# Moving the low parts of u and the block sums of u from GpSimd to VectorE, and the last token tile's transposes by twelve matmuls, in a two-layer diffusion backbone on one core

## Chip, core, metric

One core of a Trainium2 chip runs the whole program as one launch. The metric is the device time of that launch in microseconds. TensorE is PE in the profile (its weight loads are PEld), VectorE is DVE, ScalarE is ACT, GpSimd is POOL, and SP is the queue that issues most DMAs.

## What is computed

One inference step of two layers for 128 context tokens and 512 latent tokens, 640 tokens of width 1024 that share the weights. Cut to what matters here:

```
for l in range(2):
    x = LN(a*x + 0.5*g1 * SwiGLU_1(x*(1+s1) + b1))      # d_ff 2816
    x = LN(a*x + g2 * W_out[RG-LRU | GQA | MLA](x*(1+s2) + b2))
    x = LN(a*x + 0.5*g3 * SwiGLU_2(x*(1+s3) + b3))

SwiGLU(u) = (silu(u @ w_gate) * (u @ w_up)) @ w_down
```

Everything is float32. The shifts, scales and gates come from a modulation product of the condition vector. The outputs are the tokens of both groups and the context tensors of each layer.

## The kernel before, in words

**Products.** A float32 product is made of three passes: each operand is split into a high part (rounded to the type that TensorE multiplies) and a low part (the operand less its high part), and `mm3` adds hi·hi, hi·lo and lo·hi in PSUM. Weights come by SP DMAs of 512 KB into `raw` (seven buffers); ScalarE casts the high part (L195, L1063) and VectorE subtracts to get the low part (L200, L1067).

**The stage input u.** u = x*(1+s)+b is held transposed as `uh` and `ul`, each two tiles of 128 x 4 x 640 (features by tokens). `ln_b(t)` makes token tile t of it: eight transposes on TensorE (L516) into a PSUM tile of tag `p2`; eight evacuations with scale and shift into `uf`, shared between VectorE (L521) and ScalarE (L523); then for each half of the features a cast to `uh` (ScalarE, L527) and `ul = uf - uh` (L529, GpSimd). `uf` has one buffer, so tile t+1 cannot be evacuated before the low parts of tile t are done. `p2` has three slots of two banks, shared with the accumulators of gate and up.

**Order of the stages.** f00 (first FFN of layer 0, `ffn_steps`), m0 (mixer), f01, f10, m1, f11; f01, f10 and f11 are the three that `ffn_fast` writes and that the diff reaches with all its parts. They start at 884, 1340 and 2128 us. At the end of a stage, the last part runs token tile by token tile: the products of tile t, VectorE's multiply and add (L1211, L1212) and statistics (L478), `ln_a(t)` (aggregate L485, L487; a power on GpSimd, L488; the factors, L502; the normalisation on ScalarE, L506, and VectorE, L508), then `modulate(t-1)`, that is `ln_b` of the tile before. So tile 4, the last, is left over: `end_tile` puts its `modulate` into `after_q`, and the next stage's first step calls it by `after_a()`.

**Start of a fast FFN.** `first()` in `ffn_fast` runs gate columns 0 to 383 (24 matmuls, token tiles 0 to 2), then `after_a()` (tile 4's transposes and the rest of `ln_b`), up columns 0 to 383 (24 matmuls), gate columns 384 to 639 (tiles 3 and 4), up columns 384 to 639. `mtile` yields after every 12 matmuls. The mixer's `first()` has the same form and its `after_a()` is not in the diff.

**Sums and the change to seven products.** From the fourth block of d_ff on, a fast FFN computes gate and up by seven half-size products on sums of the four blocks of u (two feature halves by two token halves). `sums()` runs behind the first three blocks as a background generator: `whole` adds `uh + ul` of a block (L990, eight per FFN on GpSimd, 128x640 each), VectorE adds and subtracts these (L997, L1002, L1003, L1009), ScalarE and VectorE split them again (L985, L986). `third()` then closes the `p2` pool, opens single-bank `pb` tiles and starts the products (L1091). The multiply of gate and up (L941) of the third block must be done before the pool can be swapped. `residual` (L2351, L2352) is more VectorE background work of this stretch.

**What sets the order on an engine.** When the program is built, a scheduler orders each engine's instructions: among those whose inputs it plans to be ready, the one that stands first in the program goes first, and `high_priority(offset=n)` counts an instruction as n places earlier (`SUMS` = 200 for the sums). On the chip each engine keeps that order, whatever comes late.

**Weights of the projections.** `run` executes a list of `Step`s. Before a step's body it finishes the step's own splits (high and low parts of its weights); while the body yields, it makes splits of the nearest following steps that have any: `near` holds the first `look` of them, and `cap` is how many splits may be made ahead in this step:

```
near = [todo[k] for k in range(i + 1, min(len(steps), i + 40)) if steps[k].splits][: s.look]
cap = s.cap
for more in s.body():
    cap += more or 0
    nxt = next((q for q in near if q), None)
    if nxt and cap and self.ahead and nxt[0].ready():
        nxt.popleft()()
        cap -= 1
```

The mixer's token-major projections (`tokens`) are steps of four splits each with cap 2; the last of them adds 2 by `yield 2`. They come in the order 1024, 1280, (1504, a `proj` of two splits), 512, 768, then the MLA weights (two splits), sixteen loads of modulation weights, and the output projection.

Of the kernel before, what the change touches and what calls it, by code (L numbers as in the profile page):

```python
# [18 lines left out]
P = 128  # L19
# [5 lines left out]
CUT = 384  # L25
# [44 lines left out]
LN_LAG = 1, 1  # L70
WOUT = (0,), (1,), (2, 3)
WCAP = 1
LOV = ()
FA = 1
FIN = ()
QP = 1
# [12 lines left out]
def f(ap):  # L89
    return ap.bitcast(F32)  # L90
# [20 lines left out]
class Kern:  # L111
# [398 lines left out]
    def ln_b(self, x, t, sp, bp, uh, ul):  # L510

        nc = self.nc
        g = 1 if t == 0 else 0
        pt = self.p2().rearrange("p a (b c) -> p (a b) c", c=P)
        for k in range(KT):
            nc.tensor.transpose(pt[:, k, :], x[:, k * P : (k + 1) * P], self.ident)  # L516
        uf = self.pp.tile([P, KT, P], F32, tag="uf", bufs=1, name=self.nm("uf"))
        for k in range(KT):
            s1, s2 = sp[:, g, k : k + 1], bp[:, g, k : k + 1]
            if k % 4 < EVAC[self.ln_idx[1] != 1]:  # L520
                nc.vector.tensor_scalar(uf[:, k, :], pt[:, k, :], s1, s2, op0=ALU.mult, op1=ALU.add)  # L521
            else:
                nc.scalar.activation(uf[:, k, :], pt[:, k, :], AF.Identity, bias=s2, scale=s1)  # L523
        for h in range(2):
            d = uh[h][:, :, t * P : (t + 1) * P]
            v = uf[:, 4 * h : 4 * h + 4, :]
            nc.scalar.copy(d, v)  # L527
            e = nc.vector if (t, h) in LOV else nc.gpsimd
            e.tensor_sub(ul[h][:, :, t * P : (t + 1) * P], v, f(d))  # L529

    def u_alloc(self):
        return [self.U([P, 4, TOK]) for _ in range(2)], [self.U([P, 4, TOK]) for _ in range(2)]
# [350 lines left out]
    def ffn_fast(self, l, j, mods):  # L883
# [8 lines left out]
        nc, I = self.nc, self.I  # L892
# [5 lines left out]
        def B(dt=F32):  # L898
            return env["pool"].tile([P, TOK], dt, tag="B", bufs=10, name=self.nm("b"))
# [7 lines left out]
        def SB(shape):  # L907
            return env["pool"].tile(shape, F32R, tag="S", bufs=6, name=self.nm("s"))
# [4 lines left out]
        def view(w, m):  # L913
            return w[l, j][:, fs(m)].rearrange("(k p) f -> p k f", p=P)
# [8 lines left out]
        def split_h(m, s):  # L923
            hh, hl = B(F32R), B(F32R)
            nc.scalar.copy(hh, s)
            nc.vector.tensor_sub(hl, s, f(hh))
            hs[m] = (hh, hl)


        def plain(m):  # L930
            g, u = {}, {}
            gl, gsp = self.weight(view(I["ffn_w_gate"], m), [P, KT, P], g, self.W)
            ul, usp = self.weight(view(I["ffn_w_up"], m), [P, KT, P], u, self.W)

            def silu(cut):
                for a, b in self.chunks(g["s"], g["ps"], cut):
                    nc.scalar.activation(a, b, AF.Silu)

            def hout(cut):
                for a, b in self.chunks(g["s"], u["ps"], cut):  # L940
                    nc.vector.tensor_mul(a, a, b)  # L941
                split_h(m, g["s"])

            def first():
                env["cm"] = self.tc.tile_pool(name=f"ffn{l}{j}", bufs=1, reuse_waits="tile")
                env["pool"] = env["cm"].__enter__()
                g["ps"], u["ps"] = self.p2(), self.p2()
                g["s"] = B()
                yield from self.mtile(g["ps"], g, 0, CUT)
                self.hold = True  # L950
                self.after_a()
                yield from self.mtile(u["ps"], u, 0, CUT)
                yield from self.mtile(g["ps"], g, 1, CUT)
                silu(CUT)
                env["sums"] = sums()
                self.bg.append(env["sums"])
                yield from self.mtile(u["ps"], u, 1, CUT)
                hout(CUT)

            def gate():  # L960
                g["ps"] = self.p2()
                g["s"] = B()
                for c in range(2):
                    yield from self.mtile(g["ps"], g, c)
                silu(HALF)

            def up():
                u["ps"] = self.p2()
                for c in range(2):
                    yield from self.mtile(u["ps"], u, c)  # L970
                hout(HALF)

            if m == 0:
                return [Step([gl, ul], gsp + usp, first)]
            return [Step([gl], gsp, gate), Step([ul], usp, up)]


        def sums():
            uh, ul = self.uh, self.ul
            env["S"] = {i: (SB([P, 4, HALF]), SB([P, 4, HALF])) for i in (1, 2, 4)}  # L980
            env["s3"] = []

            def put(i, t, ks):
                hi, lo = env["S"][i]
                nc.scalar.copy(hi[:, ks], t)  # L985
                nc.vector.tensor_sub(lo[:, ks], t, f(hi[:, ks]))  # L986

            def whole(h, ts, ks):
                t = B().rearrange("p (k n) -> p k n", k=2)
                nc.gpsimd.tensor_add(t, f(uh[h][:, ks, ts]), f(ul[h][:, ks, ts]))  # L990
                return t

            for r in range(2):
                ks = slice(2 * r, 2 * r + 2)
                with self.tc.high_priority(offset=SUMS):
                    t21, t22 = whole(0, H1, ks), whole(1, H1, ks)
                    nc.vector.tensor_add(t22, t21, t22)  # L997
                yield
                with self.tc.high_priority(offset=SUMS):
                    t11 = whole(0, H0, ks)  # L1000
                    put(1, t22, ks)
                    nc.vector.tensor_sub(t21, t11, t21)  # L1002
                    nc.vector.tensor_sub(t11, t22, t11)  # L1003
                yield
                env["s3"].append((t21, ks))
                with self.tc.high_priority(offset=SUMS):
                    t12 = whole(1, H0, ks)
                    put(2, t11, ks)
                    nc.vector.tensor_sub(t12, t12, t11)  # L1009
                    put(4, t12, ks)  # L1010
                yield
# [285 lines left out]
    def mixer_steps(self, l, mods):  # L1297
        nc, I, O = self.nc, self.I, self.O
# [741 lines left out]
        def proj(c0, post, first=None):  # L2040
            h = {}
            ld, sp = self.weight(I["w_in"][l][:, c0 : c0 + P].rearrange("(k p) f -> p k f", p=P), [P, KT, P], h, self.W)
            n = len(S)

            def body():
                h["ps"] = self.p2("pg" if n % 2 == 0 else "pu")
                for c in range(2):
                    yield from self.mtile(h["ps"], h, c)
                post(h["ps"])
                yield  # L2050

            return h, ld, sp, body
# [43 lines left out]
        def tokens(c0, evac, post, pre=lambda: None, pairs=0):  # L2096

            hd = [{}, {}]
            lds, sps = [], []
            for i in range(2):  # L2100
                ld, sp = self.weight(
                    I["w_in"][l][i * 512 : (i + 1) * 512, c0 : c0 + 256].rearrange("(k p) n -> p k n", p=P),
                    [P, 4, 256],
                    hd[i],
                    self.W,
                )
                lds.append(ld)
                sps += sp

            def part(pt, t, half):  # L2110
                ts = slice(t * P, (t + 1) * P)
                for k in range(4 * half, 4 * half + 4):
                    wh, wl = hd[half]["hi"][:, k % 4, :], hd[half]["lo"][:, k % 4, :]
                    xh, xl = self.uh[half][:, k % 4, ts], self.ul[half][:, k % 4, ts]
                    self.mm3(pt, xh, xl, wh, wl, k == 0, k == KT - 1)

            def body():
                pre()
                for t in range(NT - 2 * pairs):
                    pt = self.p1()[:, 0:256]  # L2120
                    part(pt, t, 0)
                    yield
                    part(pt, t, 1)
                    evac(t, pt)
                    yield
                if pairs:
                    pts = [self.p1()[:, 0:256] for _ in range(2)]
                    part(pts[0], NT - 2, 0)
                    yield
                    part(pts[1], NT - 1, 0)  # L2130
                    yield 2
                    for i in range(2):
                        part(pts[i], NT - 2 + i, 1)
                        evac(NT - 2 + i, pts[i])
                        yield
                post()
                yield

            return Step(lds, sps, body, 2)

        def kv_evac(t, pt):
            if t == 0:
# [31 lines left out]
        for c0, post in ((128, xa1), (384, ga1)):  # L2174
            h, ld, sp, body = proj(c0, post)
# [3 lines left out]
        h, ld, sp, body = proj(1504, bgpost(c_post))  # L2179
# [407 lines left out]
```

## Time and profile before

| | us |
|---|---|
| median of 3 runs | 2592.18 |
| lowest, highest | 2592.03, 2599.52 |
| profiled execution, its own time | 2593.82 |
| its span, first to last instruction | 2592.0 |
| PE busy | 2470.4 (95%) |
| DVE busy | 1887.8 (73%) |
| ACT busy | 1067.8 (41%) |
| POOL busy | 534.6 (21%) |

In the profile a row of the timeline gives start, duration, engine, line, operation, output and inputs by name, and in brackets how long the engine was idle before it and what ended that. The windows view gives for a stretch the busy time of each engine and the mean granted TensorE clock, 1.00 for 2.4 GHz throughout and 0.50 for 1.2 GHz. The waits view sums, over the span, the time that an engine stood idle before a line, by what ended the wait, with the count and the longest. Matmuls overlap in the pipeline, so the distance between starts, not the duration, is what one costs.

### The profile page before, as it was taken

To read this page: it belongs to the slowest core of one execution; us is meant where nothing else is said; L and a number is where in the kernel's file an instruction comes from. 1 tells how busy PE (TensorE), PEld (TensorE's weight loads), DVE (VectorE), ACT (ScalarE), POOL (GpSimd) and SP (SyncE) were. 2 spreads that over 40 slices of the span, in tenths; PEclk is the share of its full clock that TensorE was granted. 3 is DMA by queue.
4 is the path that set the end of the run, shared out by engine and by line. 5 is a ranking of instruction groups with operands and counts; after the bars stand their busy time and mean duration, and the time that the engine had idled before them with its cause. 6 is when DMAs were issued, how large, how long until landed. Compare 5 with 4: busy or idle time off the path is not lost. (4 is left out here: it accounts for less than half of the span.)

```text
span 2592.0 us, 40008 instructions
## 1 busy us (share of the span) xinstructions
PE 2470.4 (95%) x15804; PEld 2220.3 (86%) x15804; DVE 1887.8 (73%) x3087; ACT 1067.8 (41%) x1882; POOL 534.6 (21%) x463
## 2 busy tenths in 40 slices
PE   7899999999999989999999999999989999999997
PEld 7689889989757989999888999988976798999986
DVE  4877768677754687777779777777785568777777
ACT  3212111246665434434353433434657534433432
POOL 2421211133622410000222000022363233000022
PEclk9999999999999999999999999999999999999999
DMA  8644446522223233333323333232331423333321
GB/s 271 211 147 146 131 129 205 155 68 78 93 88 104 73 113 100 99 113 96 109 87 112 103 97 114 91 109 76 99 117 48 135 60 112 106 90 106 121 91 49
DMA packets 271507, 288.54 MB, mean 111 GB/s; under 512 B 13548, under 2 KB 224088, under 8 KB 271320
## 3 DMA queue, kind: packets, MB, share of 16 engines
q1 hardware_dynamic: 271072, 285.91, 35.6%
q8 instruction: 124, 2.03, 0.3%
q14 instruction: 63, 0.52, 0.1%
q10 hardware_dynamic: 248, 0.08, 0.0%
HBM read 268.17 MB, written 16.21 MB: 110 GB/s over the span
## 5 line engine op out<-in xcount | busy, mean ns | idle before, releaser
L1091 PE MATMUL pb<-u,w 128*128 128x320 f32 x2736 | 422.1, 310 | 8.8 <-DVE b L941 7.2
L1091 PEld LDWEIGHTS pb<-u,w 128*128 128x128 f32 x2736 | 408.0, 188 | 11.7 <-DVE b L941 6.6
L537 PE MATMUL p<-u,w 128*128 128x320 f32 (+2 forms) x1104 | 349.3, 317 | 4.1 <-ACT uf L523 3.0
L539 PE MATMUL p<-u,w 128*128 128x320 f32 (+2 forms) x1104 | 346.4, 314 | 5.3 <-DVE w L200 5.3
L538 PE MATMUL p<-u,w 128*128 128x320 f32 (+2 forms) x1104 | 347.4, 315 | 3.3 <-POOL u L529 3.3
L1091 PE MATMUL pb<-s,w 128*128 128x320 f32 x2052 | 323.4, 311 | 4.5 <-DVE w L1067 4.0
L1091 PEld LDWEIGHTS pb<-s,w 128*128 128x128 f32 x2052 | 307.7, 189 | 6.8 <-DVE w L1067 4.5
L1063 ACT CAST w<-raw 128x512 fp32r<-128x512 f32 x399 | 240.2, 619 | 165.7 <-DVE raw L1059 110.3
L1067 DVE TENSOR_TENSOR w<-raw,w 128x512 fp32r<-128x512 f32 x399 | 271.7, 694 | 35.0 <-ACT w L1063 34.2
L195 ACT CAST dw<-raw 128x1024 fp32r<-128x1024 f32 x87 | 89.1, 1050 | 451.3 <-PE p L1204 264.9
L341 DVE SCALAR_TENSOR_TENSOR x<-raw,cst,x 128x512 f32<-128x512 f32 x308 | 235.2, 811 | 34.3 <-DMA raw<-in_w_mod 34.0
L1203 PE MATMUL p<-dw,b 128*128 128x512 f32 x630 | 250.0, 397 | 10.7 <-DVE x L1216 9.2
L1204 PE MATMUL p<-dw,b 128*128 128x512 f32 x630 | 246.2, 391 | 0.0
L1205 PE MATMUL p<-dw,b 128*128 128x512 f32 x630 | 245.9, 390 | 0.0
L537 PEld LDWEIGHTS p<-u,w 128*128 128x128 f32 x1104 | 212.0, 192 | 9.1 <-ACT uf L523 3.9
L539 PEld LDWEIGHTS p<-u,w 128*128 128x128 f32 x1104 | 211.7, 192 | 6.4 <-DVE w L200 6.4
L538 PEld LDWEIGHTS p<-u,w 128*128 128x128 f32 x1104 | 212.1, 192 | 5.4 <-POOL u L529 5.1
L195 ACT CAST w<-raw 128x1024 fp32r<-128x1024 f32 x100 | 105.0, 1050 | 245.5 <-PE p L538 176.7
L1216 DVE TENSOR_TENSOR x<-x,p 128x512 f32<-128x512 f32 x150 | 102.7, 685 | 111.4 <-PE p L1205 111.4
L1165 POOL TENSOR_SCALAR x<-x 128x1024 f32<-128x1024 f32 x6 | 6.9, 1143 | 813.5 <-DMA x<-gd 588.5
L200 DVE TENSOR_TENSOR w<-raw,w 128x1024 fp32r<-128x1024 f32 x100 | 126.9, 1271 | 56.4 <-ACT w L195 52.3
L1203 PEld LDWEIGHTS p<-dw,b 128*128 128x128 f32 x630 | 118.5, 188 | 46.1 <-DVE x L1216 20.5
(367 smaller groups left out, 4948.0 us busy)
## 6 DMA issues: line engine op xcount, KB each, us to landing
raw<-in_w_mod SPq DMA_DIRECT2D x132, 512.0 KB
raw<-in_ffn_w_gate SPq DMA_DIRECT2D x88, 512.0 KB
raw<-in_ffn_w_up SPq DMA_DIRECT2D x88, 512.0 KB
raw<-in_ffn_w_down SPq DMA_DIRECT2D x88, 512.0 KB
raw<-in_w_in SPq DMA_DIRECT2D x26, 512.0 KB
xd<-x SPq DMA_DIRECT2D x25, 512.0 KB
raw<-in_w_out SPq DMA_DIRECT2D x16, 512.0 KB
t<-xd SPq DMA_DIRECT2D x30, 256.0 KB
```

The lines of the kernel that those rows point to most:

```text
L195: nc.scalar.copy(h, hold["raw"])
L200: nc.vector.tensor_sub(l, hold["raw"], f(hold["hi"]))
L341: e.scalar_tensor_tensor(acc[:, cs], hold["raw"][:, cs], c, acc[:, cs], op0=ALU.mult, op1=ALU.add)
L537: nc.tensor.matmul(out, lhsT=wh, rhs=xh, start=start, stop=False)
L538: nc.tensor.matmul(out, lhsT=wh, rhs=xl, start=False, stop=False)
L539: nc.tensor.matmul(out, lhsT=wl, rhs=xh, start=False, stop=stop)
L1063: nc.scalar.copy(w[:, 0], at(src))
L1067: nc.vector.tensor_sub(w[:, 1], at(src), f(w[:, 0]))
L1091: nc.tensor.matmul(out, lhsT=a1, rhs=b1, start=(start and k == 0 and i == 0), stop=(k == 3 and i == 2), skip_group_check=not start,)
L1203: nc.tensor.matmul(pt, lhsT=hh[:, ts], rhs=d["hi"][:, cs], start=(i == 0), stop=False)
L1204: nc.tensor.matmul(pt, lhsT=hh[:, ts], rhs=d["lo"][:, cs], start=False, stop=False)
L1205: nc.tensor.matmul(pt, lhsT=hl[:, ts], rhs=d["hi"][:, cs], start=False, stop=(i == len(ms) - 1))
```

## The change

1. `ln_b`: both low parts of every token tile (L529) go to VectorE. 50 instructions, in all five stages that have a next stage.
2. `whole` in `sums`: the eight adds of 128x640 per fast FFN (L990) go to VectorE, 24 in all.
3. `first()` in `ffn_fast`: up's first 12 matmuls are put ahead of `after_a()`; the other 12 follow it.
4. `tokens` steps get `look=2` in place of the default 1, with the same cap.

```
@@ ln_b
             nc.scalar.copy(d, v)
-            e = nc.vector if (t, h) in LOV else nc.gpsimd
-            e.tensor_sub(ul[h][:, :, t * P : (t + 1) * P], v, f(d))
+            nc.vector.tensor_sub(ul[h][:, :, t * P : (t + 1) * P], v, f(d))
@@ first() in ffn_fast
                 self.hold = True
+                part = self.mtile(u["ps"], u, 0, CUT)
+                yield next(part)
                 self.after_a()
-                yield from self.mtile(u["ps"], u, 0, CUT)
+                yield from part
@@ whole() in sums()
-                nc.gpsimd.tensor_add(t, f(uh[h][:, ks, ts]), f(ul[h][:, ks, ts]))
+                nc.vector.tensor_add(t, f(uh[h][:, ks, ts]), f(ul[h][:, ks, ts]))
@@ tokens()
-            return Step(lds, sps, body, 2)
+            return Step(lds, sps, body, 2, look=2)
```

`LOV` was the empty tuple, so all low parts were on GpSimd before; its line is removed.

## Rows read from the trace of the kernel before

**Rows 1.** The page: busy time, share of the span, instructions of each engine.
```profile
PE 2470.4 (95%) x15804; PEld 2220.3 (86%) x15804; DVE 1887.8 (73%) x3087; ACT 1067.8 (41%) x1882; POOL 534.6 (21%) x463
```

**Rows 2.** Waits of TensorE: total us, times, longest.
```profile
PE p L516 <- ACT x L506: 13.6, 6, 4.5
...
PE p L538 <- DVE w L200: 12.0, 8, 3.0
...
PE pb L1091 <- DVE b L941: 7.2, 2, 6.2
PE p L539 <- DVE w L200: 5.3, 3, 3.9
...
PE pb L1091 <- DVE w L1067: 4.0, 2, 3.2
```

**Rows 3.** Windows: length, then busy time and instructions by engine, clock, DMA.
```profile
888.00:899.00 11.00, 7.81 (x38) 7.17 (x36) 7.53 (x15) 6.69 (x14) 6.50 (x4) 0.84 0.61 177
899.00:950.00 51.00, 43.23 (x279) 42.15 (x278) 44.06 (x54) 19.32 (x30) 17.96 (x10) 0.93 0.27 94
1310.00:1338.00 28.00, 27.98 (x135) 23.06 (x135) 23.67 (x47) 11.84 (x24) 7.74 (x9) 1.00 0.07 20
...
2144.00:2198.00 54.00, 48.49 (x318) 46.88 (x317) 50.48 (x66) 21.46 (x35) 16.83 (x9) 0.97 0.28 98
```

**Rows 4.** Timeline of TensorE: tile 4's transposes at the three fast FFNs.
```profile
890.97 1.15 PE L516 MATMUL p<-ident,x 128*128 128x128 f32 x8 [2.18 <-ACT x L506]
...
1348.87 1.97 PE L516 MATMUL p<-ident,x 128*128 128x128 f32 x8 [4.50 <-ACT x L506]
...
2135.11 0.44 PE L516 MATMUL p<-ident,x 128*128 128x128 f32 x2 [2.31 <-ACT x L506]
```

**Rows 5.** Timeline at f01's start: evacuation, low parts, TensorE's next piece.
```profile
891.51 4.64 POOL L529 TENSOR_TENSOR u<-uf,u 128x512 fp32r<-128x512 f32 x2 [1.47 <-ACT u L527]
...
893.11 0.62 ACT L527 CAST u<-uf 128x512 fp32r<-128x512 f32 x1
...
896.18 0.73 DVE L521 TENSOR_SCALAR uf<-p,sp,bp 128x128 f32<-128x128 f32 x2 [2.41 <-POOL u L529]
...
898.57 2.89 POOL L529 TENSOR_TENSOR u<-uf,u 128x512 fp32r<-128x512 f32 x2 [2.42 <-ACT u L527]
...
898.62 0.34 PE L538 MATMUL p<-u,w 128*128 128x384 f32 x1
898.79 0.33 PE L539 MATMUL p<-u,w 128*128 128x384 f32 x1
...
900.17 0.39 PE L538 MATMUL p<-u,w 128*128 128x256 f32 x1 [0.93 <-POOL u L529]
```

**Rows 6.** Groups by line over the span: busy us, mean ns, idle before.
```profile
L1067 DVE TENSOR_TENSOR w<-raw,w 128x512 fp32r<-128x512 f32 x399 | 271.7, 694 | 35.0 <-ACT w L1063 34.2
...
L529 POOL TENSOR_TENSOR u<-uf,u 128x512 fp32r<-128x512 f32 x50 | 70.9, 1420 | 56.9 <-ACT u L527 52.1 <-DVE uf L521 2.5 <-DVE spt L1495 2.2
...
L990 POOL TENSOR_TENSOR b<-u,u 128x640 f32<-128x640 f32 x24 | 48.0, 2033 | 0.8 <-DVE s L986 0.8
```

**Rows 7.** Timeline of VectorE around the first block of f11 and f10.
```profile
2147.52 1.27 DVE L200 TENSOR_TENSOR w<-raw,w 128x1024 fp32r<-128x1024 f32 x1 [4.01 <-ACT w L195]
2148.72 2.20 DVE L997 TENSOR_TENSOR b<-b,b 128x640 f32<-128x640 f32 x1
...
2162.17 0.81 DVE L997 TENSOR_TENSOR b<-b,b 128x640 f32<-128x640 f32 x1
...
1348.20 0.54 DVE L508 TENSOR_SCALAR x<-x,bnve 128x512 f32<-128x512 f32 x1
...
1361.12 1.50 DVE L200 TENSOR_TENSOR w<-raw,w 128x1024 fp32r<-128x1024 f32 x1 [5.91 <-ACT w L195]
```

**Rows 8.** Groups by line of VectorE, 1310 to 1338 us.
```profile
L508 DVE TENSOR_SCALAR x<-x,bnve 128x512 f32<-128x512 f32 x3 | 3.3, 1084 | 0.0
...
L502 DVE TENSOR_SCALAR bnve<-bnmv,bnve 128x1 f32<-128x1 f32 x4 | 0.9, 214 | 2.1 <-POOL bnve L488 2.1
```

More of the change, by code (lines that the diff above doesn't have):

```diff
@@ L72 @@
 WCAP = 1
-LOV = ()
 FA = 1
```

## The prediction

> **What bounds the kernel now.** The page comes first: TensorE is busy for 95% of the span, VectorE for 73%, GpSimd for 21% [rows 1]. So time is to be had only where TensorE stands idle, or runs at 1.2 GHz after it stood. The waits of TensorE say where the change can touch that [rows 2]. The three things to see: it waits 13.6 us for normalised tokens before the transposes of a last token tile (L516 for L506); 16.5 us in all (7.2 + 5.3 + 4.0) for VectorE in the first three blocks of a fast FFN and at its pool swap (L941, L200 at L539, L1067); and 12.0 us for projection weights in the mixers (L200 at L538). The windows view then tells what VectorE does there: 44.06 of 51 us behind the first block of f01, 50.48 of 54 in f11 [rows 3]. In those stretches VectorE, not TensorE, is the engine that ends the waits. Around the start of f01 the granted clock is 0.84, and 0.93 and 0.97 in the stretches behind the first block: TensorE stood, then ran for a while at 1.2 GHz.
>
> **Part 2, the sums (the largest term).** Removed are 24 adds on GpSimd at 2.03 us, 48.0 in all, 16 us per fast FFN [rows 6]. Added are 24 on VectorE. The like operation there, an add of two 128x640 SBUF tiles, takes 0.81 us when GpSimd is quiet and 2.20 while GpSimd makes its sums [rows 7]. So per FFN 8 x 0.81 = 6.5 us are added. What goes away: about six VectorE operations with two SBUF inputs of this size lie in the 16 us of each FFN (the first of f11's is the L997 at 2148.72), each longer by up to 1.39 us; as not all lie in it whole, I take 1.25, so 7.5 us. The Trainium skill (SBUF — State Buffer, Who interferes with whom) has it that a VectorE instruction with two SBUF inputs and a GpSimd instruction that reads SBUF exclude each other for a whole instruction; the 2.20 beside 0.81 agrees. There is also room ahead of the jam: VectorE is idle 4.01 us in f11 and 5.91 in f10 before its first weight split, since that waits for TensorE to free a buffer [rows 7], and the sums depend only on u, which is complete then. As the sums are counted 200 places earlier, they will be ordered into that gap. Net, VectorE's queue reaches the pool swap earlier by 7.5 - 6.5 + (4.0 to 5.9) = 5.0 to 6.9 us per FFN.
>
> Against that stand the waits: 16.5 us over three FFNs, 5.5 on average, the longest 6.2 [rows 2]. Each FFN has about what VectorE gains, so nearly all of it could go; I take 12, since the first product behind the swap still has its weights to wait for. The clock: (1 - 0.93) x 51 = 3.6 us in f01 and (1 - 0.97) x 54 = 1.6 in f11 [rows 3], f10 taken as f11: 6.8, part of it while TensorE stood anyway. I take 3. Sum for part 2: 15 us; bounds 0 (what VectorE gains is given back to other queued work) and 16.5 + 6.8 = 23.
>
> **Parts 1 and 3 at the start of the three fast FFNs.** TensorE waits 2.18, 4.50 and 2.31 us before tile 4's transposes, 9.0 in all [rows 4]. Part 3 puts 12 matmuls of 384 columns there; their starts are 0.17 apart [rows 5], so 2.1 us of work, which fits each hole. But what is late next is seen in f01: TensorE waits again, 0.93 us, for tile 4's low part before gate's second piece [rows 5]. That piece can't start before the chain through `uf` ends, wherever the transposes' wait is filled; with 12 matmuls less behind the transposes, the same wait shows there instead. So the move alone is worth 0 where that chain is last, and up to 2.1 where it isn't. What shortens the chain is part 1. In f01 GpSimd needs 4.64 us for tile 3's two low parts, and VectorE's evacuation of tile 4 waits for them, until 896.18 [rows 5]. The cast ahead of the second ends at 893.11 + 0.62 = 893.73; a low part on VectorE is a 128x512 subtraction, 0.69 us by L1067 [rows 6], so `uf` is free at about 894.4, 1.7 us earlier. Tile 4's own low parts take 2.89 us for two on GpSimd [rows 5] against 1.4: 0.9 earlier for the first. Together 2.6 us in f01, if VectorE is free when they are ready; it also has weight splits of over 1 us in its queue there. I take 2 us for each of the three starts: 6 us. Bounds: 0 and 9.0 plus the clock's (1 - 0.84) x 11 = 1.8 in f01 [rows 3], say 12. The moved `after_a` passes no DMA on SP. Its casts and evacuations come 2.1 us later at most, and nothing queued behind them on ScalarE is needed by TensorE before gate's second piece.
>
> The two mixer starts get part 1 alone. Tile 4's wait for normalisation stays (4.6 of the 13.6 us), the low parts behind it get faster. I take 0, bounds -2 and 3.
>
> **Part 1 at the ends of stages, a cost.** While the last products run token tile by token tile, TensorE is the bound: 27.98 of 28 us in f01's end. VectorE is at 23.67 [rows 3], for four tiles (L502 four times [rows 8]). Eight low parts add 8 x 0.69 = 5.5, so 29.2 in 28 us, were nothing else to change. What changes: L508 takes 1.08 on average there [rows 8], and 0.54 where GpSimd is quiet [rows 7] (its 3.3 us in this window would be 1.6), which brings 27.5. VectorE also idles 2.1 us on the power [rows 8], some of which the low parts can fill. So it goes from 85% to nearly full, with TensorE still just ahead. The cost is bounded by 0 and 29.2 + 2.1 - 28 = 3.3 us for each of the five ends; I take 0.5 each, near the lower bound, as the 27.5 lies below 28: 2.5 us. A low part now waits on VectorE for ScalarE's cast; queued behind it are the next product's multiply (L1211), which frees a PSUM tile for TensorE, and weight splits, which free `raw` buffers for SP's loads. The loads have slack: TensorE's list of waits names a weight's DMA at the program's start alone, and the multiply is what the 0.5 stands for.
>
> **Part 4, look=2.** It changes which splits may be made ahead only when the next step's are used up and `cap` still has some left. Step 1024 has cap 2 and four splits ahead of it; 1280 has cap 2 and the two of `proj` 1504; 512 has cap 2 and four of 768: the cap is spent on the nearest step each time. 768 has cap 2 and the two MLA splits, and gets 2 more late by `yield 2`; the next step with splits is the output projection, whose loads stand behind sixteen loads of 512 KB in a queue of seven buffers, so its first split isn't ready. So nothing moves: 0 us.
>
> **Sum.** 15 + 6 + 0 - 2.5 - 0 = 18.5 us. The profiled execution took 2593.8, the median of the runs is 2592.2, 0.06% less. So 2575.3 against the one and 2573.7 against the other; I forecast 2574.
>
> **The rivals.**
> *The wait moves only.* In the jam behind the first block VectorE also carries background work of the residual, put in wherever a slot is planned. If the queue in front of L941 is the order's doing and not VectorE's lateness, taking 7.5 us out lets other work in and TensorE waits as before. For: the 44.06 of 51 us [rows 3] leaves VectorE little room. Against: in f01 and f11 a stall follows a stretch in which its operations took 2.20 in place of 0.81. Then part 2 is worth 0: 2592.2 - 6 + 2.5 = 2589. The Trainium skill (Perfetto Trace Analysis, Optimizing Scalar/DVE Operations) says that moving work between GpSimd and VectorE might not help, since they share an SBUF read port; it would give this case, and the trace has both signs, VectorE slowed by GpSimd and a full queue on VectorE.
> *VectorE saturates (slower).* Everything added runs on the engine that ends the waits. If the operations don't get shorter, each stage end costs its upper bound, 5 x 3.3 = 16.5; the sums add 6.5 per FFN, of which about 5 fit into the idle gap, 3 x 1.5 = 4.5; and the starts gain nothing, as the chain through VectorE is longer by the low parts of two tiles. That is 2592.2 + 21 = 2613, or 2603 with half of it. It decides once VectorE's work per token tile exceeds TensorE's 7.0 us; it stands now at 23.67 / 4 = 5.9, and at 6.9 by my working.
> *look=2 does something.* Were my count of caps wrong, the projections' 12.0 us [rows 2] could go: 2574 - 12 = 2562. Against it is the code alone; no row shows it.
>
> **How the numbers follow.** A measurement of this kernel can tell about 0.3%, 7.8 us, from no change, so faster ends at 2584. My forecast has 0.60 (own range 2562 to 2588, of which 0.05 lies within 0.3%); the wait moves only 0.22 (2584 to 2597, nearly all within 0.3%); saturation 0.12 (2598 to 2613, 0.11 of it slower); look=2 0.06. That gives faster 0.64, within 0.3% 0.24, slower 0.12. The range reaches down to the sum with the upper bounds of the first two terms, 2592.2 - 23 - 12 = 2557, and up to the lower edge of saturation, 2598.
>
> **What would show it.** Right: L997, L1002, L1003 and L986 at 0.8 us throughout; the first sums right behind tile 4's low parts, with no 4 to 6 us of idle VectorE; the waits of TensorE for L941, L200 (L539) and L1067 at a third or less; the wait before tile 4's transposes shorter, with up's first 12 matmuls ahead of it; L521 no longer waiting for L529. In the stage ends TensorE still without holes and VectorE near 27 of 28. Wrong: TensorE waiting for L1211 or L838 in the stage ends; the same waits for L941 behind unslowed sums; a VectorE order in which low parts stand behind weight splits of 1.2 us; projections with other splits ahead than before.

## The result, and the profile of the changed kernel

The changed kernel takes 2566.28 us (median of 4 runs, 2564.24 to 2567.44), the kernel before beside it 2595.74 (4 runs): a ratio of 0.9886, 95% interval 0.9865 to 0.9907. The forecast was 2574, the range 2557 to 2598. The profiled execution has a span of 2562.9 us, against 2592.0: 29.1 less. Helper lines have moved a little: L515 (before L516) makes the transposes, L535 to L537 the three matmuls of a gate or up product, L505 the normalisation on ScalarE, L520 and L522 the evacuation to `uf`, L526 the cast, L527 the low parts, L199 a weight split, L830 and L836 (before L832 and L838) the first FFN's products and their multiply; from L952 on, the numbers are those of before.

The page, busy time by engine (it answers to [rows 1]):

```profile
PE 2459.3 (96%) x15804; PEld 2212.2 (86%) x15804; DVE 1892.7 (74%) x3161; ACT 1068.2 (42%) x1882; POOL 417.3 (16%) x389
```

GpSimd lost 117.3 us, and VectorE, which took this work over, gained 4.9. The next fences show how that can be. Groups by line with shapes kept apart (line, engine, operation, tiles and shapes, count; busy us, mean ns; idle before), first of before, then of after:

```profile
L986 DVE TENSOR_TENSOR s<-b,s 128x640 fp32r<-128x640 f32 x18 | 21.1, 1178 | 0.0
L508 DVE TENSOR_SCALAR x<-x,bnve 128x512 f32<-128x512 f32 x15 | 15.2, 1013 | 0.0
L2286 DVE TENSOR_TENSOR x<-x,b 128x256 f32<-128x256 f32 x20 | 12.9, 643 | 0.6
L997 DVE TENSOR_TENSOR b<-b,b 128x640 f32<-128x640 f32 x6 | 9.0, 1503 | 0.0
```

```profile
L527 DVE TENSOR_TENSOR u<-uf,u 128x512 fp32r<-128x512 f32 x50 | 34.2, 685 | 5.3 <-ACT u L526 5.3
L990 DVE TENSOR_TENSOR b<-u,u 128x640 f32<-128x640 f32 x24 | 18.7, 818 | 0.0
L986 DVE TENSOR_TENSOR s<-b,s 128x640 fp32r<-128x640 f32 x18 | 14.8, 820 | 0.0
L2286 DVE TENSOR_TENSOR x<-x,b 128x256 f32<-128x256 f32 x20 | 8.5, 423 | 0.4
L507 DVE TENSOR_SCALAR x<-x,bnve 128x512 f32<-128x512 f32 x15 | 8.1, 541 | 0.1
L997 DVE TENSOR_TENSOR b<-b,b 128x640 f32<-128x640 f32 x6 | 4.9, 820 | 0.0
```

Added are 34.2 + 18.7 = 52.9 us. The four groups of before gave back 6.3, 7.1, 4.4 and 4.1; summed over all records, VectorE's other operations are 39 us shorter. The rest of the 48 between 52.9 and 4.9 is overlap: neighbouring records overlap by 10 us more in all, and busy time counts an overlap once. So 118.9 us of GpSimd's work (70.9 and 48.0 in [rows 6]) were less than half as long on VectorE, and some three quarters of that were paid back by VectorE's other operations, which got shorter.

The waits of TensorE (total us, times, longest), which answer to [rows 2]:

```profile
PE p L830 <- DVE t L836: 13.1, 17, 1.4
PE p L536 <- DVE w L199: 10.5, 6, 3.0
PE p L1203 <- DVE x L1216: 9.6, 24, 1.0
...
PE p L535 <- ACT u L526: 7.1, 4, 2.9
PE p L515 <- ACT x L505: 6.8, 7, 2.3
```

The waits for L941, for L200 at the third matmul, and for L1067 are gone. That for the normalisation is 6.8 us in place of 13.6, the projections' is 10.5 in place of 12.0. One is nearly new: 7.1 us for the cast L526 (0.8 in before), ahead of gate's second piece. The timeline of TensorE shows where that lies, in f01, f10 and f11 (against [rows 4] and [rows 5]):

```profile
892.88 1.09 PE L515 MATMUL p<-ident,x 128*128 128x128 f32 x8 [0.81 <-ACT uf L522]
...
897.59 0.80 PE L535 MATMUL p<-u,w 128*128 128x256 f32 x2 [2.91 <-ACT u L526]
...
1343.70 0.51 PE L535 MATMUL p<-u,w 128*128 128x256 f32 x2 [1.62 <-ACT u L526]
...
2112.89 1.09 PE L515 MATMUL p<-ident,x 128*128 128x128 f32 x8 [0.80 <-ACT uf L522]
...
2118.10 0.51 PE L535 MATMUL p<-u,w 128*128 128x256 f32 x2 [2.37 <-ACT u L526]
```

Windows (length; busy time and instructions of PE, PEld, DVE, ACT, POOL; granted clock, DMA share, GB/s) behind the first block of f01 and f11, and of f01's end, against [rows 3]:

```profile
899.00:937.00 38.00, 38.00 (x248) 37.57 (x248) 33.30 (x47) 15.80 (x23) 0.00 (x0) 0.94 0.28 90
...
2122.00:2160.00 38.00, 38.00 (x259) 37.49 (x259) 34.61 (x50) 16.82 (x24) 0.00 (x0) 0.99 0.29 98
```

```profile
1302.00:1331.00 29.00, 28.11 (x134) 22.80 (x133) 26.00 (x54) 13.52 (x30) 2.92 (x4) 1.00 0.05 18
```

In both windows behind the first block TensorE now has no hole. VectorE in f11 is at 91% (34.61 of 38) where it was at 93% with TensorE waiting.

**Where the 29.1 us come from.** A stage's start is counted here, on TensorE's timeline, from the first matmul of its first product (gate, or h0 in a mixer) to the second hi·hi matmul of that product's second piece; the rest of the stage runs from there to the next stage's first matmul. All from one profiled execution of each kernel:

| us | before | part 1 alone | part 2 alone | part 3 alone | parts 1+2 | changed |
|---|---|---|---|---|---|---|
| start m0 | 16.72 | 11.47 | 16.73 | 16.74 | 11.48 | 11.46 |
| start f01 | 16.71 | 15.28 | 16.67 | 14.95 | 14.57 | 13.78 |
| start f10 | 16.75 | 11.95 | 15.74 | 15.72 | 11.96 | 11.95 |
| start m1 | 16.74 | 13.57 | 16.78 | 16.78 | 13.57 | 13.57 |
| start f11 | 14.54 | 13.09 | 14.51 | 13.93 | 13.29 | 13.09 |
| rest f01 | 439.4 | 439.3 | 430.8 | 438.8 | 431.6 | 434.0 |
| rest f10 | 437.9 | 441.0 | 432.1 | 440.3 | 434.1 | 433.4 |
| rest f11 | 449.6 | 451.2 | 442.6 | 450.3 | 443.2 | 444.6 |
| f00, rest m0, rest m1 | 1183.7 | 1181.7 | 1186.9 | 1189.0 | 1185.2 | 1187.1 |

The starts give 17.6 us (8.4 in the mixers, 9.2 in the fast FFNs), the rests of the fast FFNs 14.9; the last line takes 3.4 back. In that line single executions differ by more than the parts explain: part 3 alone changes no step of these stages and has 5.3 more.

### The profile page after: what moved, and what is told of

It is laid out like the page before. It is cut to its first block, busy times and chain, and to the rows that moved or that the text cites. A ratio compares the mean times of both kernels' runs of the same rounds, so it can differ in the third digit from the quotient of the medians.

```text
span 2562.9 us, 39968 instructions
## 1 busy us (share of the span) xinstructions
PE 2459.3 (96%) x15804; PEld 2212.2 (86%) x15804; DVE 1892.7 (74%) x3161; ACT 1068.2 (42%) x1882; POOL 417.3 (16%) x389
## 3 DMA queue, kind: packets, MB, share of 16 engines
q8 instruction: 124, 2.03, 0.3%
## 5 line engine op out<-in xcount | busy, mean ns | idle before, releaser
L535 PE MATMUL p<-u,w 128*128 128x320 f32 (+2 forms) x1104 | 347.1, 315 | 7.4 <-ACT u L526 7.1
L537 PE MATMUL p<-u,w 128*128 128x320 f32 (+2 forms) x1104 | 343.8, 312 | 0.0
L1067 DVE TENSOR_TENSOR w<-raw,w 128x512 fp32r<-128x512 f32 x399 | 272.6, 696 | 36.3 <-ACT w L1063 35.3
L535 PEld LDWEIGHTS p<-u,w 128*128 128x128 f32 x1104 | 210.4, 191 | 12.9 <-ACT u L526 8.3
L537 PEld LDWEIGHTS p<-u,w 128*128 128x128 f32 x1104 | 210.6, 191 | 0.1
L199 DVE TENSOR_TENSOR w<-raw,w 128x1024 fp32r<-128x1024 f32 x100 | 124.9, 1249 | 36.4 <-ACT w L194 32.5
```

What stands on the lines that cost most here:

```text
L199: nc.vector.tensor_sub(l, hold["raw"], f(hold["hi"]))
L535: nc.tensor.matmul(out, lhsT=wh, rhs=xh, start=start, stop=False)
L537: nc.tensor.matmul(out, lhsT=wl, rhs=xh, start=False, stop=stop)
L1067: nc.vector.tensor_sub(w[:, 1], at(src), f(w[:, 0]))
```

## Experiments

The theory: part 2's gain is VectorE's operations no longer lengthened beside GpSimd's sums, part 1's is a shorter chain through `uf` at the starts, part 3 moves a wait. Against it: that VectorE's gain is refilled (part 2 worth nothing), and that the gain is part 1's or part 3's. The first four kernels ran on one chip, beside the same runs of the kernel before (median 2597.8).

**Part 2 alone.**

```diff
-                nc.gpsimd.tensor_add(t, f(uh[h][:, ks, ts]), f(ul[h][:, ks, ts]))
+                nc.vector.tensor_add(t, f(uh[h][:, ks, ts]), f(ul[h][:, ks, ts]))
```

> Part 2 alone: the 24 adds of uh + ul on VectorE, low parts on GpSimd, after_a where it was. Theory (the adds on GpSimd slowed VectorE's own sums to 2.2 us and left it idle before the first weight split): the waits of TensorE between the start of the second gate piece and the last product behind the pool swap go, 12 to 16 us less than before in all, and the stretch from a stage's first gate matmul to its second gate piece stays at 16.7, 16.8 and 14.5 us in the three fast FFNs. Rival (the queue in front of L941 is the order's doing): the wait for L941 in f01 stays near 6 us and the time falls by less than 4 us.

Measured: 2573.83 us, 0.9908 (0.9894 to 0.9923), 24.0 less. That is more than the 12 to 16 expected. The rests of the three fast FFNs are 8.6, 5.7 and 7.0 us shorter, 21.3 in all; the starts stay, but for 1.0 in f10. Of the waits for L941, for L200 at the third matmul and for L1067 none is left, and the slow stretches behind them went with them: the granted clock behind f01's first block (901 to 952) is 1.00, where it was 0.93 [rows 3]. So the wait did not move. By the records, the 24 sums add 20.8 us to VectorE, and its other operations are 20.7 us shorter.

**Part 1 alone.**

```diff
-            e = nc.vector if (t, h) in LOV else nc.gpsimd
-            e.tensor_sub(ul[h][:, :, t * P : (t + 1) * P], v, f(d))
+            nc.vector.tensor_sub(ul[h][:, :, t * P : (t + 1) * P], v, f(d))
```

> Part 1 alone: the 50 low parts on VectorE. Theory (the chain through the single uf buffer sets when the second piece can start, in all five stage starts): starts shorter by 1 to 5 us each, 8 to 16 us in all, with the mixers' among them; the ends of stages longer by 0.5 to 2 us each, so 5 to 12 us less than before. Rival (the starts got shorter only because part 3 filled the wait with matmuls): the three fast starts stay within 1 us, the mixers' get shorter, and the time falls by 0 to 5 us. Second rival (VectorE saturates in the ends): slower than before by 5 us or more.

Measured: 2583.07 us, 0.9944 (0.9929 to 0.9959), 14.7 less. That is more than the 5 to 12 expected. All five starts are shorter, 16.1 us in all, and more than half of that, 8.4, is in the mixers. The waits of TensorE at the swap stay as long as they were or get longer; only that for L200 at the third matmul is gone:

```profile
PE pb L1090 <- DVE b L940: 8.0, 3, 5.8
PE pb L1090 <- DVE w L1066: 6.4, 2, 3.2
```

The trace of before holds m0's reason, and it is not among the rows that stand ahead of the prediction. The timeline of all engines in before at m0's start (start us, length, engine, line; in brackets the idle time before and its releaser):

```profile
553.65 0.81 ACT L506 ACTIVATE x<-x,bnve 128x512 f32<-128x512 f32 x1 [3.04 <-DVE bnve L502]
...
554.37 1.14 ACT L523 ACTIVATE uf<-p,bp,sp 128x128 f32<-128x128 f32 x3
...
554.52 1.09 PE L516 MATMUL p<-ident,x 128*128 128x128 f32 x8 [1.69 <-ACT x L506]
...
556.24 1.15 ACT L523 ACTIVATE uf<-p,bp,sp 128x128 f32<-128x128 f32 x3
556.24 1.26 POOL L529 TENSOR_TENSOR u<-uf,u 128x512 fp32r<-128x512 f32 x1 [2.52 <-DVE uf L521]
...
557.45 0.69 PE L537 MATMUL p<-u,w 128*128 128x384 f32 x1 [1.83 <-ACT uf L523]
```

and its window behind that wait:

```profile
557.40:562.40 5.00, 4.96 (x15) 4.96 (x16) 3.92 (x18) 1.44 (x4) 1.38 (x2) 0.50 0.00 0
```

The next product's first matmul needs a PSUM tile that the evacuation into `uf` has to free first; TensorE stands 1.83 us for it, right behind the 1.69 before the transposes, and then runs 5 us at a granted clock of 0.50, that is at 1.2 GHz: 2.5 us more. The same place in after:

```profile
557.86 1.09 PE L515 MATMUL p<-ident,x 128*128 128x128 f32 x8 [1.17 <-ACT x L505]
...
563.50 0.50 PE L535 MATMUL p<-u,w 128*128 128x256 f32 x2 [0.16 <-ACT u L526]
```

No wait is between the two, and the clock is 1.00 there (557.9 to 563.5). 1.83 + 2.5 + (1.69 - 1.17) = 4.9 of m0's 5.3 us.

What held the evacuation up in before is the order on ScalarE, and not GpSimd directly. Both its pieces (554.37 and 556.24) belong to tile 3. GpSimd had freed `uf` at 550.4, and VectorE's share of the evacuation ran at 551.2; but in ScalarE's queue the evacuation stands behind tile 4's normalisation, and ScalarE stood idle 3.04 us for that one's factors. With part 1 alone the first piece stands ahead of the normalisation:

```profile
547.92 1.15 ACT L523 ACTIVATE uf<-p,bp,sp 128x128 f32<-128x128 f32 x3 [2.42 <-DVE uf L521]
...
551.15 0.81 ACT L506 ACTIVATE x<-x,bnve 128x512 f32<-128x512 f32 x1
```

f10 gains by order too: in before three weight splits (L200) stand on VectorE between the stage's first matmul and tile 4's factors (L502), which come 7.8 us after it; with part 1 alone it is one split and 5.3 us. The wait before tile 4's transposes falls from 4.50 to 1.96, and the granted clock behind it, 0.50 from 1348.87 to 1354.5 in before, stays at 1.00. In f01 it is the chain itself: VectorE's evacuation of tile 4 starts 11.1 us after the stage's first matmul, not 12.4. In m1 the waits for L527 (0.80) and L529 (0.95) ahead of the second piece are gone; the rest of its 3.2 us was not taken apart. That the scheduler changed these orders because it now plans the low parts to end earlier fits its rule, but no run tests it.

**Part 3 alone.**

```diff
+                part = self.mtile(u["ps"], u, 0, CUT)
+                yield next(part)
                 self.after_a()
-                yield from self.mtile(u["ps"], u, 0, CUT)
+                yield from part
```

> Part 3 alone: up's first twelve matmuls ahead of after_a in the three fast FFNs. Theory (the chain behind tile 4's transposes is last, so the wait only moves): the wait before the transposes gets shorter by 2 us or more and a wait of about the same size appears before the second gate piece; the time falls by 0 to 4 us. Rival (the hole before the transposes was the loss): each of the three starts is shorter by 2 us or more plus the time at 1.2 GHz behind it, 6 to 12 us in all.

Measured: 2597.16 us, 0.9997 (0.9988 to 1.0007): no change. The wait moves, as f01's timeline of TensorE shows:

```profile
897.72 1.09 PE L516 MATMUL p<-ident,x 128*128 128x128 f32 x8 [1.55 <-ACT uf L523]
903.11 0.50 PE L537 MATMUL p<-u,w 128*128 128x256 f32 x2 [2.91 <-ACT u L527]
904.74 0.39 PE L538 MATMUL p<-u,w 128*128 128x256 f32 x1 [1.13 <-POOL u L529]
```

2.18 us before the transposes became 1.55, and 2.91 and 1.13 appear before the second piece, where 0.93 stood [rows 4, 5]. The starts of the three fast FFNs are 3.4 us shorter in its profiled execution all the same, but their rests are 2.6 longer, and nothing of it shows in the time.

**Parts 1 and 2, without parts 3 and 4.** The first two diffs above together.

> Parts 1 and 2 without part 3. If the parts add up and the changed kernel's 29 us are starts 17.6, stretch behind the first block 14.8 and ends -3.3, this has all but part 3's share of the three fast starts: 20 to 27 us less than before. Rival (part 3 and the low parts need each other at the fast starts): only the mixers' starts keep their 8 us, 17 to 20 us less than before.

Measured: 2559.13 us, 0.9852 (0.9837 to 0.9867), 38.7 less than before, where 20 to 27 were expected: just 24.0 + 14.7. The two parts add. The wait for the normalisation is 13.6 us here, as in before, so the changed kernel's 6.8 is part 3's doing. This is under the changed kernel's 0.9886, so the two were also put side by side.

**The changed kernel, and parts 1 and 2 again, on one chip.** Both as they stand above.

> The changed kernel once more, beside the one without part 3 on the same chip. Theory (part 3 costs: it adds nothing to the starts of f10 and f11 that part 1 hasn't given, and makes the stretch behind the second gate piece of f01 and f11 longer): 2 to 9 us slower than the kernel of parts 1 and 2. Rival (the two differ by chip alone): within 2 us of it.

> Parts 1 and 2 without part 3, on the chip of the run of all parts. Theory: 35 to 40 us less than before, as in the first run, 2 to 9 us less than all parts. Rival: within 2 us of all parts.

Measured (before: 2597.96): the changed kernel 2564.85, 0.9869 (0.9854 to 0.9884); parts 1 and 2 alone 2561.19, 0.9855 (0.9839 to 0.9871). Twice the version without parts 3 and 4 has the lower ratio, by 3.7 us here, but the intervals overlap: that part 3 costs something beside the others is likely and not settled. The profiled executions have the difference in f01 and f11: rests of 433.5 and 444.8 for the changed kernel, 431.7 and 443.6 for parts 1 and 2. In f01 the wait of 2.85 us stands before the transposes without part 3, and 2.91 before the second piece with it; so it buys nothing. Behind the moved wait the granted clock is 0.94 (899 to 937, above), and 0.95 in the changed kernel's second trace; without part 3 it is 1.00 in the same stretch of both traces. Part 4 is no part of this difference: by line, operation and tile, the instructions of the two kernels stand in the same order on every engine and on SP, but for the three groups of eight transposes that part 3 moves.

**Giving the contention back: parts 1 and 2 with GpSimd adds that nobody reads.** Behind each sum on VectorE, GpSimd makes it too, in four adds of 128x160 into a tile that isn't used.

```diff
+                z = env["pool"].tile([P, 160], F32, tag="Z", bufs=1, name=self.nm("z"))
+                for k in (ks.start, ks.start + 1):
+                    for c in (0, 160):
+                        cs = slice(ts.start + c, ts.start + c + 160)
+                        nc.gpsimd.tensor_add(z, f(uh[h][:, k, cs]), f(ul[h][:, k, cs]))
```

> Parts 1 and 2, and on top GpSimd makes the adds of uh + ul as well, in four pieces of 128x160 each into a tile that nobody reads; VectorE's work is that of parts 1 and 2. Theory (GpSimd's reads lengthen VectorE's two-input operations): L997, L1002, L1003 and L986 at up to 2.2 us again while GpSimd adds, the waits of TensorE behind the first block come back in part, 5 to 15 us slower than parts 1 and 2. Rival (the gain came from the adds standing in the idle gap of VectorE and from their earlier end): VectorE's operations at 0.8 us and the time within 3 us of parts 1 and 2.

Measured: 2592.46 us, 0.9972 (0.9961 to 0.9984): 31.3 above parts 1 and 2 on the same chip, where 5 to 15 were expected. Every engine but GpSimd has its instructions in the order of parts 1 and 2. Groups by line with shapes apart:

```profile
L1207 PE MATMUL p<-dw,b 128*128 128x512 f32 x630 | 252.3, 401 | 9.9 <-DVE x L1220 8.9 <-DVE t L1215 1.1
L1209 PE MATMUL p<-dw,b 128*128 128x512 f32 x630 | 248.6, 395 | 0.0
L1208 PE MATMUL p<-dw,b 128*128 128x512 f32 x630 | 248.3, 394 | 0.0
...
L994 POOL TENSOR_TENSOR z<-u,u 128x160 f32<-128x160 f32 x96 | 91.7, 955 | 28.1 <-DVE u L528 18.8 <-PE p L516 2.2
...
L1001 DVE TENSOR_TENSOR b<-b,b 128x640 f32<-128x640 f32 x6 | 6.9, 1150 | 0.0
```

Where VectorE's adds took 0.82 they take 1.15, and the wait for weight splits at the third matmul, 5.3 us in before and gone in after, is back (those for the multiply and at the swap are not):

```profile
PE p L538 <- DVE w L200: 12.9, 3, 6.0
```

But the rows of L1207 to L1209, the down products' matmuls, are longer too: 749.2 us against 740.8 of parts 1 and 2 (second run of it):

```profile
L1202 PE MATMUL p<-dw,b 128*128 128x512 f32 x630 | 249.7, 396 | 11.1 <-DVE x L1215 9.9 <-DVE t L1210 1.2
L1203 PE MATMUL p<-dw,b 128*128 128x512 f32 x630 | 245.7, 390 | 0.0
L1204 PE MATMUL p<-dw,b 128*128 128x512 f32 x630 | 245.4, 390 | 0.0
```

So this run had a second difference, of some 8.4 us, which isn't VectorE's. That is what the next kernels are for.

**The same with memsets in place of the adds.** GpSimd writes `z` eight times per sum (`ZN` is 8), and reads SBUF for one column only.

```diff
+                z = env["pool"].tile([P, 160], F32, tag="Z", bufs=1, name=self.nm("z"))
+                nc.gpsimd.tensor_copy(z[:, 0:1], f(ul[h][:, ks.start, ts])[:, 0:1])
+                for _ in range(ZN):
+                    nc.gpsimd.memset(z, 0.0)
```

> Parts 1 and 2, and on top eight memsets of 128x160 per sum on GpSimd in place of adds, each lot behind a copy of one column of ul so that it falls at the same time: GpSimd writes SBUF and reads none of it but that column. Theory (what lengthens VectorE's operations is GpSimd's reading): L997, L1002, L1003 and L986 stay at 0.8 us and the time is within 3 us of parts 1 and 2. Rival (any GpSimd work beside VectorE slows it): as with the adds.

Measured: 2571.73 us, 0.9895 (0.9879 to 0.9910), 10.5 above parts 1 and 2, where at most 3 were expected. VectorE's adds take 0.82 (L1001: 816 ns), beside 46.9 us of memsets, and the three matmul groups take 749.4 us:

```profile
L1207 PE MATMUL p<-dw,b 128*128 128x512 f32 x630 | 252.3, 400 | 10.5 <-DVE x L1220 8.1 <-ACT x L1212 1.2 <-DVE t L1215 1.0
L1209 PE MATMUL p<-dw,b 128*128 128x512 f32 x630 | 248.8, 395 | 0.0
L1208 PE MATMUL p<-dw,b 128*128 128x512 f32 x630 | 248.3, 394 | 0.0
...
L994 POOL MEMSET z<- 128x160 f32 x192 | 46.9, 244 | 10.9
```

Not all of the adds have memsets beside them, but of the 48 sums and their adds and subtractions (L990, L1001, L1006, L1007, L1013) 19 have, for more than half of their time, and these too take 0.82. So GpSimd's reads lengthen VectorE's adds and its writes don't. The Trainium skill (SBUF — State Buffer, Who interferes with whom) says that a VectorE instruction with two SBUF inputs contends with a GpSimd instruction that reads SBUF, "not with one that only writes it"; 1.15 and 0.82 agree. And the matmuls' 8.6 us are there without any lengthening of VectorE.

**The tile alone, in two sizes.** No memset: once with the tile of 160 columns, once with `[P, 64]` in its place.

```diff
-ZN = 8
+ZN = 0
```

> Parts 1 and 2 with the unread tile of 128x160 of the GpSimd runs allocated in the same place, and only the copies of one column on GpSimd, no memsets and no adds. Theory (the tile shifts others of the pool in SBUF, and the 1800 matmuls of 512 columns in the fast FFNs start 232 in place of 227 ns apart): the same 232 ns, 7 to 10 us slower than parts 1 and 2. Rival (GpSimd's memsets lengthened them): 227 ns and within 3 us of parts 1 and 2.

> As the run before with a tile of 128x64. If the placing of tiles in SBUF sets the distance of the 512-column matmuls, it may differ from both: 227 ns and no loss, 232 ns and 7 to 10 us, or less than 227 ns and a gain. If the tile's size plays no part: as the run before.

Measured (another chip, before: 2596.71): 160 columns 2567.29, 0.9895 (0.9881 to 0.9910); 64 columns 2562.23, 0.9876 (0.9854 to 0.9897). The same group of the two kernels:

```profile
L1207 PE MATMUL p<-dw,b 128*128 128x512 f32 x630 | 252.5, 401 | 10.0 <-DVE x L1220 8.8 <-DVE t L1215 1.1
```

```profile
L1207 PE MATMUL p<-dw,b 128*128 128x512 f32 x630 | 249.9, 397 | 11.0 <-DVE x L1220 9.8 <-DVE t L1215 1.2
```

The three groups together take 749.8 and 741.5 us, and the rests of the three fast FFNs differ by 7.9; every engine has the same order of instructions in both. The times differ by 5 us, with intervals that overlap. An unread tile of 640 bytes a partition is enough to lengthen the matmuls, one of 256 bytes isn't. That a new tile in the pool shifts the places of those behind it is the likely reason, but which tile's place does it was not looked for. So what GpSimd's adds cost is read against kernels with the same tile: 20.7 us against the memsets on the same chip (where a few instructions of f10 stand in another order), and 0.9972 against 0.9895, that is 20 us, against the tile alone. The 66 lengthened sums, adds and subtractions of VectorE (L986, L990, L997 and their like in before's lines) are 20.7 us longer by their records, 0.31 each.

**Only the last tiles' low parts on VectorE.** If part 1's gain is the last tiles' chain, and its cost the first tiles' load at the stage ends, this keeps the gain and saves the cost.

```diff
-            nc.vector.tensor_sub(ul[h][:, :, t * P : (t + 1) * P], v, f(d))
+            e = nc.vector if t >= 2 else nc.gpsimd
+            e.tensor_sub(ul[h][:, :, t * P : (t + 1) * P], v, f(d))
```

> Part 2, and part 1 for token tiles 2, 3 and 4 alone: the low parts of tiles 0 and 1 stay on GpSimd, where TensorE is still busy with the last products. Theory (only the last tiles' chain reaches TensorE, the first tiles' low parts on VectorE are cost): starts as with parts 1 and 2 (11.5 to 14.6 us), the ends of stages 0.3 to 1 us shorter each, 2 to 4 us less than parts 1 and 2, 38 to 42 us less than before. Rival (the ends cost nothing): within 1.5 us of parts 1 and 2.

Measured: 2568.58 us, 0.9893 (0.9879 to 0.9908), against 0.9855 and 0.9852 with all tiles. From the last down matmul to the next stage's first takes 1.20 and 1.24 us behind f01 and f10 here, 2.12 and 2.11 with all low parts on VectorE, 1.45 and 1.48 in before. So the ends do pay, 0.65 us each at this place. But the starts of m0, f10 and m1 are 2.9, 3.7 and 3.1 us longer than with all tiles: in m0 TensorE waits 2.78 before the transposes, not 1.17, and the granted clock falls behind it (0.88 from 553 to 567). The time is 28.1 us under before, where 38 to 42 were expected. The idea fell.

**Part 3's move in the mixers too.** The changed kernel, with h1's product split in the same way in the mixers' first step.

```diff
+            part = self.mtile(h1["ps"], h1, 0, CUT)
+            yield next(part)
...
-            yield from self.mtile(h1["ps"], h1, 0, CUT)
+            yield from part
```

> All parts, and part 3's move in the mixers' first step too. Theory (the chain through uf ends last at a start, wherever matmuls stand): the mixers' starts stay at 11.5 and 13.6 us within 0.5, the time within 2 us of all parts. Rival (the waits of 1.2 and 2.3 us before their transposes are the loss): each of the two starts shorter by 1 to 2 us, 2 to 4 us less than all parts.

Measured: 2570.15 us, 0.9906 (0.9890 to 0.9923), no better than the changed kernel's 0.9886 and 0.9869. m0's start stays at 11.47, m1's goes from 13.57 to 12.60; but the kernels with memsets and with the 64-column tile, without this move, have 12.62 and 12.61 there, so that gain is not shown to be the move's.

## Why the prediction was right, and where its terms were off

The sign, the range and the mechanism of part 2 held; the time came 8 us under the forecast, as three terms were too small. The range held by its width: the mixers' term lies outside its own bounds, and the upper bounds of the two terms that set the range's lower end were not reached.

- **Part 2, 15 us: measured 21.3.** The mechanism is shown twice: the operations fall to 0.82, and reads by GpSimd alone bring back 20 to 21 us. What was too careful is the step "I take 12" of 16.5 and "I take 3" of 6.8. All three waits went, and with them the stretches at 1.2 GHz behind them; the measured value is next to the upper bound of 23. The count of what gets shorter, 7.5 us per FFN, was about right: 20.7 in all with part 2 alone, 18.0 of it in L986, L997, L1002, L1003 and L1009. L508 and L2286 are not part of this; they get shorter with part 1 alone and stay as they were with part 2 alone.
- **The starts of the fast FFNs, 6 us: measured 9.2** in the changed kernel (2.9, 4.8, 1.5), 7.7 by part 1 alone. f01 and f11 gain less than the 2 us each by part 1 alone (1.4 and 1.5). f10 is the one that was mis-sized: the 2 us were worked out on f01's chain and carried over. Its own wait of 4.50 us [rows 4] was for VectorE's factors behind three weight splits; it fell by 2.5 with the order on VectorE, and the 5.6 us at a granted clock of 0.50 behind it, which the bound counted for f01 alone, went with it.
- **The mixers' starts, "I take 0": measured 8.4.** This is the step that failed outright. The bounds were -2 and 3. The prediction looked at the transposes' wait and went no further along TensorE's timeline; in m0 the next wait, 1.83 us for L523, has 1.2 GHz behind it, and goes when ScalarE's order changes. In the list of waits this line stood low, and nothing in it tells the clock. The prediction took the orders on the engines as fixed; part 1 changed them.
- **Part 3, worth 0 where the chain is last: right.** It is 0.9997 alone, and its wait shows where the prediction said, before gate's second piece. That part 1 then makes the move pay did not happen: the starts of f01 are 13.78 and 13.41 with it and 14.57 and 13.75 without.
- **The stage ends, 2.5 us: about right in size, not in place.** 0.65 us shows at the ends of f01 and f10; the rests of the fast FFNs say 3.3 us in all for part 1 beside part 2 (0.8, 2.0, 0.6), with variation of the same size. The prediction put the cost at the next product's multiply (L1211); that wait is 1.2 us in both kernels. What waits is the transposes of tile 3, 0.88 us for their normalisation, behind f01 and behind f10, where before had no wait. VectorE is at 26.00 of 29 us, under the 27 of 28 that was worked out, but that window holds five of the eight low parts that were counted.
- **look=2, 0 us: right**, by the order of the instructions: with it and without it the order differs in part 3's transposes alone.
- **The rivals.** That the wait only moves fell with part 2 alone (24 us less). Saturation fell with part 1 alone: VectorE takes on 50 operations of 0.7 us, is 10.7 us busier, and the kernel is 14.7 us faster. The Trainium skill (Perfetto Trace Analysis, Optimizing Scalar/DVE Operations) says that moving work between these two engines might not help. Here it helped: 118.9 us left GpSimd and VectorE gained 4.9, as GpSimd's reads no longer lengthened VectorE's operations.

In sum: 21.3 + 17.6 is 38.9 us. Part 1's cost in the rests takes 3.3 back, part 3's 3.1 (434.0, 433.4, 444.6 against 431.6, 434.1, 443.2), and the last line of the table 3.4, which leaves the span's 29.1. These terms are differences between columns of one table, so they must add up; what shows that the parts add is the separate times, 24.0 + 14.7 against 38.7. For the 3.4 no cause is claimed.

What the prediction asked of the profile came out: the sums' operations at 0.82, and the first sums right behind tile 4's low parts with no idle VectorE, as VectorE's timeline in f11 shows (f01 is alike; in f10 only one sum stands there, and then 1.1 us of idle time and a weight split):

```profile
2120.30 0.69 DVE L527 TENSOR_TENSOR u<-uf,u 128x512 fp32r<-128x512 f32 x1 [0.53 <-ACT u L526]
2120.91 2.29 DVE L990 TENSOR_TENSOR b<-u,u 128x640 f32<-128x640 f32 x3
2123.12 0.82 DVE L997 TENSOR_TENSOR b<-b,b 128x640 f32<-128x640 f32 x1
```

**Still open.** What part 3 costs beside part 1 (3.7 us, overlapping intervals); which tile's place lengthens the matmuls; why the scheduler's order changed with part 1. The fastest version seen is parts 1 and 2 without the rest: 0.9852 and 0.9855.

## What to carry to other kernels

Work on GpSimd is not free because GpSimd is idle: look at the same VectorE line at quiet and at busy times, and charge the lengthening of all VectorE operations in the stretch to GpSimd's instruction; here the bill for the sums (20.7 us) was as large as the sums themselves on VectorE (20.8). Follow TensorE's timeline past a late chain's first wait to each later one, and add the granted clock behind each. Look at what stands ahead in the queue of the engine that ends a wait: moving work to another engine can change that order, and in two of the five starts most of the gain came from it. A move of work into a hole is worth nothing while what ends the hole is also what the next step needs: shorten the chain instead.

## What the runs showed of the hardware that was not expected

- An unread tile of 640 bytes a partition in the pool made 1890 matmuls of 512 columns take 749 to 750 us in place of 741, mean 394 to 401 ns by group in place of 390 to 397, in three kernels, with quiet and with busy GpSimd; one of 256 bytes did not. A probe that adds a tile has to be read with that in mind.
- Lengthening beside GpSimd isn't for adds of two tiles alone: L508, an operation with one 128x512 input and per-partition scalars, took 1.01 us on average in before and 0.54 in after. In before it took 1.27 to 1.37 in the nine cases with GpSimd's L529 beside it, and 0.54 to 0.55 in the six without.
- The lengthening depends on GpSimd's instruction: beside its adds of 128x640 (2.03 us) a VectorE add took up to 2.20 us, beside adds of 128x160 (0.96 us) at most 1.16.
